# An S5 layer on one Trainium2 core: T products moved between the state inputs, a scan of every fourth step with expansion, and E fetched earlier

## The chip, the cores and the metric

The kernel runs on one core of a Trainium2 chip. The metric is the time of the program on the device in microseconds (us). TensorE (PE) multiplies matrices, VectorE (DVE) and ScalarE (ACT) work element by element on 128 partitions, GpSimd (POOL) does a few side jobs, SyncE (SP) issues nearly all DMA transfers, one after the other in program order. Every engine has its own in-order stream, and semaphores join the streams.

## The reference, cut to what matters

The reference is a network of two blocks over 512 tokens of width 1024. The first block (sparse and dilated attention, cross attention, MLP) and the odd layer of the second are not touched by the change. The part in question is the S5 layer of the even mixer, a linear recurrence in both directions over 256 context and 512 latent steps, for 48 groups of 16 channels and 64 complex states:

```python
def s5_direction(u, lam_re, lam_im, log_step, b_re, b_im, c_re, c_im):
    ...
    lam_bar = jnp.exp(lam * step)
    bu = lax.complex(jnp.einsum('btgh,gph->btgp', u, b_bar.real),
                     jnp.einsum('btgh,gph->btgp', u, b_bar.imag))
    a = jnp.broadcast_to(lam_bar, bu.shape)
    _, s = lax.associative_scan(_linear_recurrence, (a, bu), axis=1)
    return (jnp.einsum('btgp,ghp->btgh', s.real, c_re.astype(f32))
            - jnp.einsum('btgp,ghp->btgh', s.imag, c_im.astype(f32)))
```

Then `even_branch_out` applies gelu and a gated product to the sum of both directions, an FFT mix to the other 256 channels (`ub`), multiplies by `silu(z)` and projects with `even_w_out`.

## The kernel before, in words

The kernel works on chunks of 8 steps, so the recurrence has 96 chunk steps (32 of context, 64 of latents) in each direction. `even` (the S5 layer) runs in this order around the change:

- `U` holds the inputs, three tiles of 16 groups each (a third). They come from transposes of `UC` (L837).
- State inputs ("win products"): 24 pairs of groups `gp`, 16 products each (L1207), of `U` and a weight tile `win` of 512 KB that serves two pairs and is fetched by SP just ahead in the loop (L1201). All results go to banks named `sc`. They are copied into the states `St` by ScalarE (L1213) or, for every odd pair of the first 16, by VectorE (L1211).
- `tree` builds the states of the first 32 chunk steps in five levels of VectorE operations (L1192 to L1195), for 16 pairs at once and then for 8.
- `scan` takes the other 64 chunk steps one by one, 8 VectorE operations of 128x48 each (L1229 to L1235). It is issued at a low priority (`behind(3000)`), so the scheduler, which sets each engine's order when the program is built, lets the weight splits `wlo` (L138) of the products that follow go between its steps.
- Meanwhile TensorE does the product for `ub` (columns 768 to 1024 of `even_w_in`), the four 256-column pieces of the `z` product and the FFT products (`k_dft`).
- `T`: three tiles of 1 MB, the in-chunk response. Each is fetched by 8 DMAs of 16 partitions, in runs of 128 float32 (512 B); they are issued behind the `z` product (L1261). The T products (L1317, 32 matrix instructions in the trace per third) come after the first half of an `even_w_out` product and are copied to `YC` by ScalarE (L1318).
- `E`: six tiles of 1 MB in long runs, fetched inside the loop of the E products (L1333). The E products (L1341) multiply the finished states by `E` and add to `YC` on VectorE (L1346).

The tiles `U`, `UC`, `T`, `E` and `sz` share one pool of nine buffers (`b8`); `win`, `tree`, `YC` and others share a pool of small tiles (`t4`). A load waits until the buffer it reuses has had its last reader, and, since SP's loads report on eight semaphore lanes in turn, until the load that used its lane last has landed. Every weight tile of a product is fetched as `raw` (L131), split into `whi` by ScalarE (L137) and `wlo` by VectorE (L138). A side generator in `self.sides` is advanced by `self.step()`, which `gemm_ch` calls once per weight tile.

Of the kernel before, what the change touches and what calls it, by code (L numbers as in the profile page):

```python
# [83 lines left out]
class Net:  # L84
# [817 lines left out]
    def s5_tables(self):  # L902
# [89 lines left out]
        for j in range(4):  # L992
# [170 lines left out]
    def even(self, hT, U, vpool):  # L1163
# [12 lines left out]

        def tree(g0, gn):

            mt = [self.t4k("tree"), self.t4k("tree")]
            for lev in range(5):  # L1180
                h = 1 << lev
                n = 16 // h
                for d in range(2):
                    m1, m2 = mt[d][:, :4 * n * gn].rearrange("p (k m r g) -> k p m r g", k=2, m=n, r=2)
                    to = lambda t: t.to_broadcast([128, n, 2, gn])
                    if lev:
                        P3 = self.s5P[:, lev - 1, :, d * 24 + g0:d * 24 + g0 + gn]
                        a, b = to(P3[:, None, 0:1]), to(P3[:, None, 1:3])
                    else:
                        a, b = [to(t[:, None, d, :, g0:g0 + gn]) for t in (self.s5A, self.s5B)]  # L1190
                    dst = steps(d, 2 * h - 1, 2 * h, n, g0, gn, False)
                    V.tensor_mul(m1, a, steps(d, h - 1, 2 * h, n, g0, gn, False))  # L1192
                    V.tensor_mul(m2, b, steps(d, h - 1, 2 * h, n, g0, gn, True))
                    V.tensor_add(m1, m1, dst)
                    V.tensor_add(dst, m1, m2)  # L1195

        for gp in range(24):
            o, l = divmod(gp, 8)
            if gp % 2 == 0:
                win = self.t4k("win").rearrange("p (j d r n) -> p j d r n", j=2, d=2, r=2)  # L1200
                nc.sync.dma_start(win, self.WinD[:, gp:gp + 2])  # L1201
            p = self.bank("sc", 2)[:, :384].rearrange("p (r n) -> p r n", r=4)
            for d in range(2):
                for r in range(2):
                    for g in range(2):
                        u = 64 * (g ^ gp % 2)
                        nc.tensor.matmul(p[u:u + 64, 2 * d + r], win[:, gp % 2, d, r, 64 * g:64 * g + 64],  # L1207
                                         U[o][:, 8 * g + l, 32 * d:32 * d + 96], start=True, stop=True)
            dst = St[:, :, :, :, gp].rearrange("p s d r -> p (d r) s")
            if gp % 2 and gp < 16:  # L1210
                V.tensor_copy(dst, p)  # L1211
            else:
                nc.scalar.activation(dst, p, AF.Copy)  # L1213
        tree(0, 16)
        tree(16, 8)

# [8 lines left out]
        mt = self.const.tile([128, 192], F32, name="scan").rearrange("p (d m r g) -> d m p r g", d=2, m=2, r=2)  # L1225
        with self.behind(3000):
            for j in range(32, 96):
                for d in range(2):
                    V.tensor_mul(mt[d][0], self.s5A[:, d], at(d, j - 1))  # L1229
                for d in range(2):  # L1230
                    V.tensor_mul(mt[d][1], self.s5B[:, d], at(d, j - 1, swap=True))
# [22 lines left out]
        self.gemm_ch(hT, W, zc[3:] + zc[:3], e_z)  # L1254
        Ts = []
        for o in range(3):
            T = self.b8("T", (128, 16, 128))
            for k in range(8):
                src = bass.AP(tensor=self.WD.tensor, offset=self.WD.offset + o * 16 * 3840 + (7 - k) * 16,
                              ap=[[240, 16], [3840, 16], [1, 128]])  # L1260
                nc.sync.dma_start(T[k * 16:(k + 1) * 16], src)  # L1261
            Ts.append(T)
        yf = [self.t4.tile([128, 2, 512], F32R, tag="t4", name=self.nm("yf")) for _ in range(2)]
# [44 lines left out]

        YCs = []
        for o, T in enumerate(Ts):  # L1310
            YCs.append(self.t4k("YC").rearrange("p (k l h) -> p k l h", k=8, h=16))
            for l0 in (0, 4):
                p = self.bank("sc", 2).rearrange("p (l n) -> p l n", l=4)
                for l in range(4):
                    for g in range(2):
                        k = 8 * g + l0 + l
                        nc.tensor.matmul(p[64 * g:64 * g + 64, l], U[o][:, k, 32:96], T[:, k], start=True, stop=True)  # L1317
                nc.scalar.activation(YCs[o][:, :, l0:l0 + 4].rearrange("p k l h -> p l k h"),  # L1318
                                     p.rearrange("p l (k h) -> p l k h", h=16), AF.Copy)

        gate = self.row(self.adaD[0, 2 * D:3 * D], self.t4k("gate"))

        self.gemm_tok([(yf[0][:, m], yf[1][:, m]) for m in range(2)], A["even_w_out_2"][0][768:], cols(0, D, 512), self.gated(gate))


        ga = []
        for o in range(3):
            YC = YCs[o]
            for l0 in (0, 4):

                ps = [b[:, :256].rearrange("p (l n) -> p l n", l=2) for b in (self.bank("sc", 2), self.mm())]
                E = self.b8("E", (128, 4, 2, 2, 128))
                nc.sync.dma_start(E, self.ED[:, o * 8 + l0:o * 8 + l0 + 4])  # L1333
                for j0 in (0, 2):
# [183 lines left out]
```

## Time and profile before

| | us |
|---|---|
| median of 3 runs | 1365.66 (1363.42 to 1372.89) |
| the profiled execution | 1365.85 |
| its span from first to last instruction | 1364.1 |
| PE busy, share | 1299.4, 95% |
| DVE busy, share | 987.8, 72% |
| ACT busy, share | 557.0, 41% |
| TensorE clock granted, mean over the span | 0.989 of full |

All times below are microseconds from the start of the span of the profiled execution. In a timeline row the two first numbers are start and length, "xN" says how many instructions are drawn together, and the bracket gives the idle time before the row and what ended it. In a row by windows each engine has its busy time and its instructions; then come the granted clock, the mean busy share of the 16 DMA engines (packets that overlap on an engine can take it above 1) and the rate.

### The profile page before, as it was taken

The page shows a single profiled execution, that of the slowest core. Times are in us where ns is not written, and L with a number is a line of the kernel's source. Part 1 is how long each engine was busy: PE and PEld are TensorE (multiplying, and loading weights), DVE is VectorE, ACT ScalarE, POOL GpSimd, SP SyncE. Part 2 cuts the span into 40 slices and gives each one's busy share as a digit, 9 for nine tenths or more (in the row PEclk, how much of TensorE's full clock was granted, in tenths as well). Part 3 has the DMA queues.
Part 4 walks back from the last instruction along what each step waited for, and adds up shares of the span by engine and source line. Part 5 has one row for each costly group of instructions (what it writes and reads, how often), then busy time and mean ns, then how long its engine had stood idle before and what let it go on. Part 6 is the DMA issues. An engine that isn't in the chain of part 4 may idle for free.

```text
span 1364.1 us, 21183 instructions
## 1 busy us (share of the span) xinstructions
PE 1299.4 (95%) x8106; PEld 1079.8 (79%) x8106; DVE 987.8 (72%) x2284; ACT 557.0 (41%) x992; POOL 71.6 (5%) x135
## 2 busy tenths in 40 slices
PE   5999999999999999999999999979999789999997
PEld 5999577578888888787887887879888678787886
DVE  6998897868966454897999955692499966623545
ACT  5533643554526243433433434552433254333222
POOL 2000000021000010000000001010000000200000
PEclk9999998999999999999999999989999899999999
DMA  6422001055752236534677764551316925321321
GB/s 211 124 63 93 32 1 62 31 183 164 271 203 94 93 74 175 186 108 157 200 210 208 225 197 139 186 152 50 110 54 80 292 94 162 105 93 62 125 92 62
DMA packets 151877, 178.07 MB, mean 131 GB/s; under 512 B 27124, under 2 KB 118490, under 8 KB 151008
## 3 DMA queue, kind: packets, MB, share of 16 engines
q1 hardware_dynamic: 148560, 168.17, 40.3%
q0 software_dynamic: 3216, 8.56, 2.0%
q8 instruction: 64, 1.05, 0.3%
q14 instruction: 37, 0.30, 0.1%
HBM read 161.24 MB, written 15.45 MB: 130 GB/s over the span
## 4 chain that ended last, share of the span: by engine, by line
PE 58%; DVE 9%; ACT 3%; issue 2%; DMA 2%; POOL 1%; SPq 0%; DVEq 0%; POOLq 0%; ACTq 0%
PE mm L175 17%; PE mm L177 16%; PE mm L176 16%; DVE wlo L138 2%; PE pv L682 1%; PE sc L1082 1%; DMA ctx<-ctx_dram 1%; DVE h L317 1%; PE sc L1207 1%; PE tr L299 1%; ACT h L277 1%; PE tr L1064 1%; ACT whi L137 1%; DMA T<-WD 1%; DVE h L319 1%
## 5 line engine op out<-in xcount | busy, mean ns | idle before, releaser
L138 DVE TENSOR_TENSOR wlo<-raw,whi 128x1024 fp32r<-128x1024 f32 (+2 forms) x197 | 230.1, 1185 | 118.4 <-ACT whi L137 118.2
L137 ACT ACTIVATE whi<-raw 128x1024 fp32r<-128x1024 f32 (+2 forms) x197 | 198.5, 1027 | 285.2 <-PE mm L176 114.3
L175 PE MATMUL mm<-hmh,whi 128*128 128x512 f32 (+1 forms) x288 | 106.4, 370 | 0.0
L176 PE MATMUL mm<-hml,whi 128*128 128x512 f32 (+1 forms) x288 | 105.4, 366 | 0.0
L177 PE MATMUL mm<-hmh,wlo 128*128 128x512 f32 (+1 forms) x288 | 105.3, 366 | 0.0
L175 PE MATMUL mm<-whi,ah 128*128 128x512 f32 x256 | 101.3, 398 | 2.3 <-DVE x L618 2.3
L177 PE MATMUL mm<-whi,al 128*128 128x512 f32 x256 | 99.5, 391 | 0.2
L176 PE MATMUL mm<-wlo,ah 128*128 128x512 f32 x256 | 99.4, 390 | 0.0
L175 PE MATMUL mm<-whi,hTh 128*128 128x256 f32 (+1 forms) x304 | 88.3, 290 | 3.5 <-ACT whi L137 2.9
L176 PE MATMUL mm<-wlo,hTh 128*128 128x256 f32 (+1 forms) x304 | 86.8, 286 | 0.0
L177 PE MATMUL mm<-whi,hTl 128*128 128x256 f32 (+1 forms) x304 | 86.6, 285 | 0.0
L618 DVE TENSOR_TENSOR x<-mm,x 128x512 f32<-128x512 f32 x87 | 58.8, 688 | 29.8 <-PE mm L177 29.3
L779 DVE SCALAR_TENSOR_TENSOR adas<-adaw,cond,adas 128x1024 f32<-128x1024 f32 x56 | 70.7, 1280 | 10.4 <-DMA adaw<-ada_w_dram 10.3
L175 PE MATMUL mm<-h2h,whi 128*128 128x512 f32 x160 | 62.8, 392 | 0.0
L176 PE MATMUL mm<-h2l,whi 128*128 128x512 f32 x160 | 62.3, 389 | 0.0
L177 PE MATMUL mm<-h2h,wlo 128*128 128x512 f32 x160 | 62.3, 389 | 0.0
L175 PEld LDWEIGHTS mm<-whi,hTh 128*128 128x128 f32 x304 | 58.6, 193 | 4.6 <-ACT whi L137 3.3
L175 PEld LDWEIGHTS mm<-hmh,whi 128*128 128x128 f32 x288 | 54.3, 189 | 9.6 <-issue 1.0
L175 PEld LDWEIGHTS mm<-whi,ah 128*128 128x128 f32 x256 | 48.0, 188 | 17.3 <-DVE x L618 4.7
L177 PEld LDWEIGHTS mm<-hmh,wlo 128*128 128x128 f32 x288 | 54.3, 189 | 8.9
L176 PEld LDWEIGHTS mm<-hml,whi 128*128 128x128 f32 x288 | 54.4, 189 | 8.4
L176 PEld LDWEIGHTS mm<-wlo,hTh 128*128 128x128 f32 x304 | 58.4, 192 | 1.6 <-issue 1.5
(515 smaller groups left out, 3302.1 us busy)
## 6 DMA issues: line engine op xcount, KB each, us to landing
adaw<-ada_w_dram SPq DMA_DIRECT2D x48, 512.0 KB
raw<-w_up_dram SPq DMA_DIRECT2D x16, 1024.0 KB
raw<-w_down_dram SPq DMA_DIRECT2D x16, 1024.0 KB
raw<-odd_w_in_dram SPq DMA_DIRECT2D x12, 1024.0 KB
raw<-w_in_dram SPq DMA_DIRECT2D x11, 1024.0 KB
raw<-w_kv_cross_dram SPq DMA_DIRECT2D x8, 1024.0 KB
raw<-even_w_in_dram SPq DMA_DIRECT2D x8, 1024.0 KB
WinD<-wst SPq DMA_DIRECT2D x24, 256.0 KB
```

The costliest lines, as they stand in the source:

```text
L137: nc.scalar.activation(hi[:, k], raw[:, k], AF.Copy)
L138: nc.vector.tensor_sub(lo[:, k], raw[:, k], hi[:, k].bitcast(F32))
L175: nc.tensor.matmul(out, lh, rh, start=(first and i == 0), stop=False)
L176: nc.tensor.matmul(out, lh, rl, start=False, stop=False)
L177: nc.tensor.matmul(out, ll, rh, start=False, stop=(final and i == n - 1))
L277: nc.scalar.activation(junk, x, AF.Square, scale=1.0 / math.sqrt(n), accum_out=ss)
L299: nc.tensor.transpose(p[:, k], h[:, (k0 + k) * 128:(k0 + k + 1) * 128], self.ident)
L317: nc.vector.scalar_tensor_tensor(h, x, r, g, op0=OP.mult, op1=OP.mult)
L319: nc.vector.tensor_add(h, h, shift)
L618: self.nc.vector.tensor_add(self.x[i][:, c:c + n], p, self.x[i][:, c:c + n])
L682: nc.tensor.matmul(o[0][:, 2 * (h % 2) + k], self.vc[:, j, c:c + 128], pt[:, j * 128:(j + 1) * 128], start=(j == 0), stop=(j == 1))
L779: nc.vector.scalar_tensor_tensor(acc[v], w, cond[:, v, k:k + 1], acc[v], op0=OP.mult, op1=OP.add)
```

## The change

The loop over the 24 pairs now holds more. All results are copied by ScalarE. Every odd pair uses a bank of the `mm` kind. After each 4 pairs `join(0, ...)` adds to every second step its left neighbour times the transition (8 operations of 128x384), after each 8 pairs `join(1, ...)` does the same for every fourth step with sums of two; 72 operations in all. After each 8 pairs the T products of that third follow at once. T tiles 0 and 1 are issued ahead of the loop, T tile 2 behind pair 13, the first three E tiles behind the loop, the other three behind the `z` product. The scan covers only every fourth step (23 steps of 8 operations with the same 128x48 shape, the transition taken to its fourth power) and runs as a side generator in pieces; then an expansion in three pieces fills the steps between (24 operations of 128x256 and 24 of 128x512). One `self.step()` is added to the FFT loop, and what is left of the generator is drained ahead of the E products. The powers of the transition are kept for two levels instead of four, in another pool; the `t4` pool has 13 buffers instead of 12; a scratch area for software DMAs is set to 8192.

```diff
-        self.t4 = P("t4", 12)
+        self.t4 = P("t4", 13)
...
-        self.s5P = self.t4k("s5P")[:, :576].rearrange("p (j r n) -> p j r n", j=4, r=3)
+        self.s5P = self.const.tile([128, 288], F32, name="s5P").rearrange("p (j r n) -> p j r n", j=2, r=3)
...
-        def tree(g0, gn):
-            mt = [self.t4k("tree"), self.t4k("tree")]
-            for lev in range(5):
...
+        def join(lev, j0, n, g0, gn):
+            h = 1 << lev
+            for d in range(2):
+                m1, m2 = jt[d][:, :4 * n * gn].rearrange("p (k m r g) -> k p m r g", k=2, m=n, r=2)
...
+                dst = steps(d, j0, 2 * h, n, g0, gn, False)
+                V.tensor_mul(m1, a, steps(d, j0 - h, 2 * h, n, g0, gn, False))
+                V.tensor_mul(m2, b, steps(d, j0 - h, 2 * h, n, g0, gn, True))
+                V.tensor_add(m1, m1, dst)
+                V.tensor_add(dst, m1, m2)
+        def t_load(o):
+            T = self.b8("T", (128, 16, 128))
+            for k in range(8):
...
+                nc.sync.dma_start(T[k * 16:(k + 1) * 16], src)
+        def e_load(n):
+            E = self.b8("E", (128, 4, 2, 2, 128))
+            nc.sync.dma_start(E, self.ED[:, 4 * n:4 * n + 4])
+        Ts = [t_load(o) for o in range(2)]
         for gp in range(24):
...
-            p = self.bank("sc", 2)[:, :384].rearrange("p (r n) -> p r n", r=4)
+            p = (self.mm() if gp % 2 else self.bank("sc", 2))[:, :384].rearrange("p (r n) -> p r n", r=4)
...
-            if gp % 2 and gp < 16:
-                V.tensor_copy(dst, p)
-            else:
-                nc.scalar.activation(dst, p, AF.Copy)
-        tree(0, 16)
-        tree(16, 8)
+            nc.scalar.activation(dst, p, AF.Copy)
+            if gp % 4 == 3:
+                join(0, 1, 48, gp - 3, 4)
+            if l == 7:
+                join(1, 3, 24, gp - 7, 8)
+                T = Ts[o]
...
+                            nc.tensor.matmul(p[64 * g:64 * g + 64, l], U[o][:, k, 32:96], T[:, k], start=True, stop=True)
...
+            if gp == 13:
+                Ts.append(t_load(2))
+        Es = [e_load(n) for n in range(3)]
...
-        with self.behind(3000):
-            for j in range(32, 96):
...
+        def scan():
+            for j in range(7, 96, 4):
...
+                if j % 32 == 7:
+                    yield
+            yield
+            for g0 in (0, 8, 16):
+                join(1, 33, 16, g0, 8)
+                join(0, 32, 32, g0, 8)
+                yield
+        self.sides.append(scan())
...
         self.gemm_ch(hT, W, zc[3:] + zc[:3], e_z)
-        Ts = []
-        for o in range(3):
-            T = self.b8("T", (128, 16, 128))
...
+        Es += [e_load(n) for n in range(3, 6)]
...
             wh, wl = self.wload(A["k_dft"], 4, (a, b))
+            self.step()
...
-        YCs = []
-        for o, T in enumerate(Ts):
...
+        for _ in self.sides.pop():
+            pass
...
-    nc = bacc.Bacc("TRN2", target_bir_lowering=False, num_devices=1)
+    nc = bacc.Bacc("TRN2", target_bir_lowering=False, num_devices=1, dynamic_dma_scratch_size=8192)
```

The first place is SP's order of loads. Before, from the last `win` tiles of the loop (`win_9563` and `win_9585` serve pairs 20 to 23) to the first E tile:

```order
L1201 DMA win_9563<-WinD 128x1024
L1201 DMA win_9585<-WinD 128x1024
L131 DMA raw_10452<-even_w_in_dram 128x8x256
L131 DMA raw_10512<-even_w_in_dram 128x8x256
L131 DMA raw_10615<-k_dft_dram 128x4x258
L131 DMA raw_10652<-k_dft_dram 128x4x256
L131 DMA raw_10780<-even_w_out_dram 128x2x512
L1261 DMA T_10572<-WD 16x16x128 x8
L1261 DMA T_10581<-WD 16x16x128 x8
L1261 DMA T_10590<-WD 16x16x128 x8
L131 DMA raw_10826<-even_w_out_dram 128x2x512
L1333 DMA E_10874<-ED 128x2048
```

Now, from the second `win` tile (pairs 2 and 3) on; `win_9405` serves pairs 4 and 5, `win_9569` pairs 14 and 15, `win_9628` pairs 16 and 17:

```order
L1215 DMA win_9375<-WinD 128x1024
...
L1201 DMA T_9335<-WD 16x16x128 x8
L1201 DMA T_9344<-WD 16x16x128 x8
L1215 DMA win_9405<-WinD 128x1024
L1215 DMA win_9427<-WinD 128x1024
L131 DMA raw_10152<-even_w_in_dram 128x8x256
...
L1215 DMA win_9538<-WinD 128x1024
L1201 DMA T_9560<-WD 16x16x128 x8
L1215 DMA win_9569<-WinD 128x1024
L1206 DMA E_9761<-ED 128x2048
L1215 DMA win_9628<-WinD 128x1024
```

Two T tiles now stand between the `win` tiles of pair 3 and pair 4, one between those of pair 13 and pair 14, and an E tile between those of pair 15 and pair 16. The second T tile (`T_9344`) waits for the last transpose of the third `U` tile (`tr_9318` below), because it takes the buffer of the `UC` tile that this transpose reads; the third (`T_9560`) waits for the T products of the first third (`mm_9476` below), whose T tile it replaces.

The second place is TensorE's order. Before, the T products stood behind the first half of `even_w_out` (its last product is the first row):

```order
L177 MATMUL mm_10806<-whi_10781,yf_10600 128x512
L1317 MATMUL sc_10716<-T_10572,U_8664 64x128 x8
L1317 MATMUL sc_10726<-T_10572,U_8664 64x128 x8
L1317 MATMUL sc_10737<-T_10581,U_8665 64x128 x8
L1317 MATMUL sc_10747<-T_10581,U_8665 64x128 x8
L1317 MATMUL sc_10758<-T_10590,U_8666 64x128 x8
L1317 MATMUL sc_10768<-T_10590,U_8666 64x128 x8
L1341 MATMUL sc_10872<-E_10874,St 64x128 x16
```

Now, from pair 1 to pair 8 (L1221 are the state inputs, L1238 the T products):

```order
L1221 MATMUL mm_9365<-U_8654,win_9353 64x96 x2
L837 MATMUL tr_9308<-ident,UC_9199 128x64 x8
L837 MATMUL tr_9318<-ident,UC_9199 128x64 x8
L1221 MATMUL mm_9365<-U_8654,win_9353 64x96 x6
L1221 MATMUL sc_9377<-U_8654,win_9375 64x96 x8
L1221 MATMUL mm_9387<-U_8654,win_9375 64x96 x8
L1221 MATMUL sc_9407<-U_8654,win_9405 64x96 x8
...
L1221 MATMUL mm_9439<-U_8654,win_9427 64x96 x8
L1238 MATMUL mm_9466<-T_9335,U_8654 64x128 x8
L1238 MATMUL mm_9476<-T_9335,U_8654 64x128 x8
L1221 MATMUL sc_9488<-U_8655,win_9486 64x96 x8
```

The T products of a third now follow its eight pairs, and the transposes that free the second T tile's buffer stand inside pair 1, where they stood before too.

## Rows read from the trace of the kernel before

**Rows 1.** By windows, from the last state inputs to the first E products.

```profile
core 0: us, PE busy (x) PEld busy (x) DVE busy (x) ACT busy (x) POOL busy (x), PEclk, DMA share, GB/s
984.00:1080.00 96.00, 85.55 (x605) 73.22 (x603) 95.19 (x612) 35.04 (x58) 3.60 (x7) 0.96 0.57 107
```

**Rows 2.** Waits of PE, 960 to 1104: us in total, times, longest.

```profile
PE sc L1317 <- DMA raw<-even_w_out_dram: 4.3, 1, 4.3
PE sc L1341 <- DVE St L1235: 2.0, 1, 2.0
PE sc L1341 <- issue: 1.0, 1, 1.0
PE mm L175 <- DVE gt L1133: 0.7, 1, 0.7
```

**Rows 3.** Timeline of PE: state inputs, behind z, T products, last E product.

```profile
967.45 1.05 PE L1207 MATMUL sc<-U,win 128*64 128x96 f32 x20
968.44 1.22 PE L837 MATMUL tr<-ident,UC 64*128 64x64 f32 x16
980.67 10.01 PE L1207 MATMUL sc<-U,win 128*64 128x96 f32 x176 [0.15 <-DVE St L1211]
...
1045.18 1.05 PE L1275 MATMUL tr<-fw 128*128 128x128 f32 x8
...
1065.55 3.76 PE L1317 MATMUL sc<-T,U 128*64 128x128 f32 x64
1073.58 3.26 PE L1317 MATMUL sc<-T,U 128*64 128x128 f32 x32 [4.27 <-DMA raw<-even_w_out_dram]
...
1102.41 0.29 PE L1341 MATMUL mm<-E,St 64*64 64x128 f32 x1
```

**Rows 4.** Timeline of SP's queue: the issue of loads.

```profile
927.55 50.77 SPq L1201 DMA_DIRECT2D win<-WinD  x6
...
1042.43 21.73 SPq L1261 DMA_DIRECT2D T<-WD  x24
1064.64 0.39 SPq L131 DMA_DIRECT2D raw<-even_w_out_dram  x1
1065.98 11.20 SPq L1333 DMA_DIRECT2D E<-ED  x6
```

**Rows 5.** By windows (columns as in Rows 1): clock, DMA share, rate.

```profile
960.00:970.00 10.00, 10.00 (x109) 9.66 (x109) 2.37 (x4) 3.20 (x7) 0.00 (x0) 1.00 0.00 0
980.00:982.00 2.00, 1.84 (x42) 1.56 (x38) 1.02 (x2) 0.84 (x1) 0.00 (x0) 1.00 0.96 338
908.00:912.00 4.00, 2.67 (x12) 2.70 (x13) 3.94 (x5) 0.00 (x0) 0.00 (x0) 0.50 0.59 167
1044.00:1062.00 18.00, 14.25 (x85) 12.27 (x85) 17.66 (x115) 7.91 (x19) 0.57 (x1) 0.96 1.27 117
1066.00:1072.00 6.00, 3.31 (x60) 2.98 (x56) 6.00 (x51) 2.39 (x4) 0.00 (x0) 1.00 1.23 130
1072.00:1090.00 18.00, 13.74 (x118) 11.72 (x120) 18.00 (x82) 2.14 (x3) 0.00 (x0) 0.91 1.02 406
```

**Rows 6.** Timeline of DVE: two tree operations; one step of the scan apart.

```profile
984.31 0.69 DVE L1192 TENSOR_TENSOR tree<-s5A,St 128x512 f32<-128x512 f32 x1
984.92 0.68 DVE L1193 TENSOR_TENSOR tree<-s5B,St 128x512 f32<-128x512 f32 x1
...
1069.84 0.33 DVE L1235 TENSOR_TENSOR St<-scan 128x48 f32<-128x48 f32 x2
...
1070.80 0.33 DVE L1235 TENSOR_TENSOR St<-scan 128x48 f32<-128x48 f32 x2
```

**Rows 7.** Groups by line on ACT, 967 to 1104: busy, mean ns | idle before.

```profile
L1213 ACT ACTIVATE St<-sc 128x384 f32<-128x384 f32 x16 | 13.7, 856 | 7.8 <-PE sc L1207 7.3
```

**Rows 8.** Timeline of PE: two waits ahead of the stretch.

```profile
852.96 0.30 PE L299 MATMUL tr<-ident,h 128*128 128x128 f32 x1 [1.47 <-DVE h L319]
...
909.33 0.55 PE L175 MATMUL mm<-whi,cxh 128*128 128x256 f32 x1 [6.46 <-DVE UC L813]
```

More of the change, by code (lines that the diff above doesn't have):

```diff
@@ L987, in s5_tables @@
         V.tensor_copy(self.s5B[:, :, 1], l8[:, 1])
-        self.s5P = self.t4k("s5P")[:, :576].rearrange("p (j r n) -> p j r n", j=4, r=3)
+        self.s5P = self.const.tile([128, 288], F32, name="s5P").rearrange("p (j r n) -> p j r n", j=2, r=3)
         re, im = sw[:, 0], sw[:, 1]
         x = t[:, :48]
-        for j in range(4):
+        for j in range(2):
             a, b, c = (self.s5P[:, j, k] for k in range(3))
@@ L1175, in steps @@
             return bass.AP(tensor=fl.tensor, offset=fl.offset + a + (24 if swap else 0), ap=ap)
-        def tree(g0, gn):
-            mt = [self.t4k("tree"), self.t4k("tree")]
-            for lev in range(5):
[L1181 to L1188, printed above, removed]
-                    else:
[L1190 to L1195, printed above, removed]
+        jt = [self.t4k("join") for _ in range(2)]
@@ new lines, in join @@
+        def join(lev, j0, n, g0, gn):
+            h = 1 << lev
+            for d in range(2):
+                m1, m2 = jt[d][:, :4 * n * gn].rearrange("p (k m r g) -> k p m r g", k=2, m=n, r=2)
+                to = lambda t: t.to_broadcast([128, n, 2, gn])
+                if lev:
+                    P3 = self.s5P[:, lev - 1, :, d * 24 + g0:d * 24 + g0 + gn]
+                    a, b = to(P3[:, None, 0:1]), to(P3[:, None, 1:3])
+                else:
+                    a, b = [to(t[:, None, d, :, g0:g0 + gn]) for t in (self.s5A, self.s5B)]
+                dst = steps(d, j0, 2 * h, n, g0, gn, False)
[3 more added lines that the diff above has]
+                V.tensor_add(dst, m1, m2)
@@ new lines, in t_load @@
+        def t_load(o):
+            T = self.b8("T", (128, 16, 128))
+            for k in range(8):
+                src = bass.AP(tensor=self.WD.tensor, offset=self.WD.offset + o * 16 * 3840 + (7 - k) * 16,
+                              ap=[[240, 16], [3840, 16], [1, 128]])
+                nc.sync.dma_start(T[k * 16:(k + 1) * 16], src)
+            return T
+        def e_load(n):
+            E = self.b8("E", (128, 4, 2, 2, 128))
+            nc.sync.dma_start(E, self.ED[:, 4 * n:4 * n + 4])
+            return E
@@ L1197, in even @@
+        Ts = [t_load(o) for o in range(2)]
+        YCs = []
         for gp in range(24):
@@ L1209, in even @@
             dst = St[:, :, :, :, gp].rearrange("p s d r -> p (d r) s")
-            if gp % 2 and gp < 16:
-                V.tensor_copy(dst, p)
-            else:
-                nc.scalar.activation(dst, p, AF.Copy)
-        tree(0, 16)
-        tree(16, 8)
+            nc.scalar.activation(dst, p, AF.Copy)
[4 more added lines that the diff above has]
+                T = Ts[o]
+                YCs.append(self.t4k("YC").rearrange("p (k l h) -> p k l h", k=8, h=16))
+                for l0 in (0, 4):
+                    p = self.mm().rearrange("p (l n) -> p l n", l=4)
+                    for l in range(4):
+                        for g in range(2):
+                            k = 8 * g + l0 + l
+                            nc.tensor.matmul(p[64 * g:64 * g + 64, l], U[o][:, k, 32:96], T[:, k], start=True, stop=True)
+                    nc.scalar.activation(YCs[o][:, :, l0:l0 + 4].rearrange("p k l h -> p l k h"),
+                                         p.rearrange("p l (k h) -> p l k h", h=16), AF.Copy)
+            if gp == 13:
+                Ts.append(t_load(2))
+        Es = [e_load(n) for n in range(3)]
         def at(d, j, swap=False):
@@ L1225, in even @@
         mt = self.const.tile([128, 192], F32, name="scan").rearrange("p (d m r g) -> d m p r g", d=2, m=2, r=2)
-        with self.behind(3000):
-            for j in range(32, 96):
+        A4 = [self.s5P[:, 1, :, d * 24:d * 24 + 24] for d in range(2)]
+        def scan():
+            for j in range(7, 96, 4):
                 for d in range(2):
-                    V.tensor_mul(mt[d][0], self.s5A[:, d], at(d, j - 1))
+                    V.tensor_mul(mt[d][0], A4[d][:, 0:1].to_broadcast([128, 2, 24]), at(d, j - 4))
                 for d in range(2):
-                    V.tensor_mul(mt[d][1], self.s5B[:, d], at(d, j - 1, swap=True))
+                    V.tensor_mul(mt[d][1], A4[d][:, 1:3], at(d, j - 4, swap=True))
                 for d in range(2):
@@ L1306, in even @@
             self.split(*self.nat(t, yf[0][:, m], yf[1][:, m]))
-        YCs = []
-        for o, T in enumerate(Ts):
[L1311 to L1319, printed above, removed]
         gate = self.row(self.adaD[0, 2 * D:3 * D], self.t4k("gate"))
         self.gemm_tok([(yf[0][:, m], yf[1][:, m]) for m in range(2)], A["even_w_out_2"][0][768:], cols(0, D, 512), self.gated(gate))
+        for _ in self.sides.pop():
+            pass
         ga = []
```

8 lines of the change are left out of this document (1 added, 7 removed).

## The prediction, made blind

> **What bounds the kernel now.** The page comes first: TensorE is the busiest engine by far over the span (table above). So a change pays only where TensorE waits, and costs wherever it makes TensorE wait. The windows of the layer in question show why the average misleads: from 984 to 1080 VectorE is busy for 95.2 of 96 us, TensorE for 85.6 [rows 1]. Then the waits of TensorE in that layer: 4.3 us ahead of the last T products, put down to a weight load, 2.0 us ahead of the first E product for the last scan step, 1.0 and 0.7 us behind it [rows 2]. The timeline gives the places: state inputs from 967.45 to 990.7 without a DMA wait, T products at 1065.55 and 1073.58, the last E product ending at 1102.7 [rows 3]. I count the result as the shift of that end; what follows it is the same work. All durations come from one profiled execution of 1365.85 us (span 1364.1), 0.2 us from the median 1365.66.
>
> **What the change takes away.** Between 1065.55 and the second `even_w_out` half stand T products of 3.76 + 3.26 us and waits of 4.27, 2.0 and 0.7 [rows 2, 3]: 14.0 us. The E tiles, issued from 1065.98 on [rows 4], are there earlier, so the 1.0 us wait goes too; later E tiles can bring another 0 to 2, and I take 1: 16 us. From the end of the state inputs (980.67 + 10.01 = 990.7) to the last E product (1102.7) [rows 3] are 112 us; 96 are left (95 to 97).
>
> **What it adds on TensorE.** The T products now stand among the state inputs. The 64 at full clock took 3.76 us [rows 3], so 96 take 5.6. Without any new wait the phase would end at 990.7 + 5.6 = 996.3 and the E products at 1092.3, 10.4 us earlier.
>
> **What it adds on VectorE.** An operation of 128x512 takes 0.61 us of its queue (984.31 to 984.92), a scan step of eight 128x48 operations 0.96 (1069.84 to 1070.80), so 0.12 each [rows 6]. Between these, 128x384 is 0.475 and 128x256 0.34. Joins: 72 x 0.475 = 34 us. Scan: 23 x 0.96 = 22. Expansion: 24 x 0.34 + 24 x 0.61 = 23. Sum 79. Before: eight copies, the tree (984.3 to 1003.1) and 64 x 0.96 = 61 of scan, about 87. VectorE saves 8 us and can begin at about 972 instead of 984, since joins start behind four pairs. The states are then ready about when the FFT products end, not behind them: the 2.0 us wait has its cover. The copies all go to ScalarE at 0.86 us [rows 7], less than the 0.91 us of a pair (176 instructions, 11 pairs, in 10.0 us [rows 3]): nothing, as long as no weight split of ScalarE's falls between two; if one does, a pair is late by about 1 us, within the range.
>
> **What it adds on SP's queue.** This decides. `win` loads were issued long ahead (six by 978.3 [rows 4]), and TensorE never waited for one. Now two T tiles stand ahead of the one for pair 4. How long is a T tile of 1 MB? While T tiles fill the queue the 16 DMA engines show a share of 1.23 to 1.27, that is full, at 117 and 130 GB/s, while the E tiles run at 406 with a share of 1.02, and `win` reached 338 [rows 5]. So 8.1 to 9.0 us per T tile, 2.6 per E tile, 1.6 per `win` of 512 KB. And later loads stand behind: the 512 KB issued at 1064.64 [rows 4] released TensorE only at 1073.58 [rows 3], when T had drained.
>
> *First stop.* T tile 0 takes the buffer of an earlier `UC` tile and runs through the quiet stretch ahead (share 0.00 from 960 to 970 [rows 5]). T tile 1 reuses a `UC` tile whose last transpose ends at 968.44 + 1.22 = 969.7 [rows 3]. Its issue takes 8 x 0.45, data flow about 1.5 us after the first issue (issues from 1042.43, a full queue from 1044 [rows 4, 5]): 971.2 to 979.3 or 980.2. `win` of pair 4 lands at 981 to 982. TensorE has done pairs 0 to 3 and the transposes at 967.45 + 4 x 0.91 + 1.2 = 972.3. It stands 8.5 to 9.5 us.
>
> *Second stop.* T tile 2 waits for the T products of the first third: 981.5 + 4 x 0.91 + 1.9 = 987, up to 989 at a low clock. On the ring stand one `win`, a 1 MB weight tile and three `win` (3.1 MB at 338 to 406 GB/s: until 989 to 991), then T tile 2 until 997 to 1000, then `win` of pair 14 at 999 to 1001.6. TensorE comes there at 992.5 to 994.5. It stands 5.5 to 8 us. The `win` of pair 16 lies behind an E tile: 2.6 + 1.6 us later, while TensorE has 1.8 + 1.9 us of work: 0.5 us.
>
> The three stops, 9 + 6.8 + 0.5 = 16.3 us at the middle (14.5 to 18), put the end of the phase at 1012.6 and that of the E products at 1108.6 instead of 1102.7. VectorE loses nothing by it. The last pair ends 1.9 us of T products ahead of 1012.6, and its copy (0.86) and 16 joins (7.6) end at 1019.2; nine scan steps (8.6) and a weight split of 2048 columns (4 x 0.61 = 2.4) end at 1030. That split, for the second piece of `z`, stands behind those nine steps in VectorE's order. The product for `ub` and the four pieces of `z` have as many columns each and fill 990.7 to 1045.2 [rows 3], 10.9 us each: TensorE needs the split at 1012.6 + 21.8 = 1034.4.
>
> **Elsewhere.** The second context tile no longer waits for a buffer that the first holds, so the 1.47 us wait at 852.96 [rows 8] may go: 0 to 1.5, taken as 1. Smaller powers, another pool, the scratch size: no instruction on this path, nothing.
>
> **The sum.** -10.4 + 16.3 - 1 = +4.9: 1365.85 + 4.9 = 1371, and 1367 to 1374 with the bounds above (stops 14.5 to 18, rest 95 to 97, context 0 to 1.5).
>
> **The rivals.**
>
> *No stop, or half.* If T tiles move faster than the rows say, or the `win` packets overtake them, up to 15 us of the stops go: 1365.85 - 10.4 - 1 = 1354, with other waits among the E products gone 1351. For it: before, T shared the queue with other loads in part of its time. Against it: even with little else the rate was 117 to 130 GB/s. [...]
>
> *VectorE becomes the bound.* The first joins read and write in runs of four numbers; the tree had 8 and 16, which no row here tells for four. If such an operation took twice as long (0.95), the 64 of them that follow pair 7 (first third done at 986) would end at 1047 instead of 1019, the split for the second `z` piece at 1058, and TensorE, needing it at 1034, would stand some 20 us at most, since later splits keep the same distance: 1391, slower. It decides from about 0.59 us per operation on (986 + 64 x 0.59 = 1024, and 11 us to the split). Against it: the tree's two widths differ as their element counts do. [...]
>
> [...]
>
> **Chances.** Both stops (1363 to 1376) 0.54; one or both halved (1357 to 1363) 0.13; none (1349 to 1356) 0.17, half of it under 1352; stops with clock (1376 to 1384) 0.10, half of it above 1379.3; VectorE 0.06. The range 1354 to 1380 leaves out about 0.2. Faster or slower by 1% (13.7 us, what a measurement of this kernel can tell): faster 0.09, slower 0.11, same 0.80.
>
> **What would show it.** In the trace after: the state inputs stretched from 23 us to 40 or more, with TensorE waiting on the DMA of `win` ahead of pairs 4 and 14; `win` landing right behind T; a DMA share above 1 at some 120 GB/s near 971 to 980; no T products behind `even_w_out`; the E products without the 4.3 and 2.0 us waits; VectorE's joins near 0.475 us. I am wrong if `win` lands within 2 us of its need (then 1354), or if a weight split on VectorE is waited for in the `z` product.

## The result: 0.9% slower, and the profile after

| | before | changed |
|---|---|---|
| median of the runs | 1365.22 us (1363.25 to 1372.89) | 1376.87 us (1374.02 to 1384.69), 7 runs |
| the profiled execution, its span | 1365.85, 1364.1 | 1375.64, 1373.5 |
| TensorE clock granted, mean | 0.989 | 0.982 |

The ratio is 1.009, with a 95% interval of 1.0069 to 1.0112. The forecast was 1371 in a range of 1354 to 1380, "same" within 1%. The time lies in the range, but 0.9 us above the likeliest case (1363 to 1376) and in the band of the rival "stops with clock" (1376 to 1384, chance 0.10). In the profiles the shift is +9.4 us where the sum had +4.9.

The waits of TensorE from 960 to 1104 in the changed kernel (us in total, times, longest) answer to [rows 2]:

```profile
PE sc L1221 <- DMA win<-WinD: 19.8, 3, 10.6
PE mm L176 <- DVE wlo L138: 3.5, 1, 3.5
PE mm L175 <- ACT yf L309: 0.3, 1, 0.3
```

The four old waits are gone. The loads of `win`, which TensorE never waited for, now stop it three times. The timeline of TensorE shows where [rows 3, 8 answer to it]; L1221 are the state inputs, L1238 the T products, L1307 the first work behind `z`, the last row is the first work of the next layer:

```profile
850.50 1.11 PE L299 MATMUL tr<-ident,h 128*128 128x128 f32 x4 [2.28 <-DVE cxl L310]
...
969.92 0.88 PE L1221 MATMUL sc<-U,win 128*64 128x96 f32 x16
...
984.73 1.55 PE L1221 MATMUL sc<-U,win 128*64 128x96 f32 x16 [10.64 <-DMA win<-WinD]
...
989.88 2.09 PE L1238 MATMUL mm<-T,U 128*64 128x128 f32 x32
991.78 0.84 PE L1221 MATMUL sc<-U,win 128*64 128x96 f32 x16
992.44 0.84 PE L1221 MATMUL mm<-U,win 128*64 128x96 f32 x16
...
995.26 0.88 PE L1221 MATMUL sc<-U,win 128*64 128x96 f32 x16 [0.65 <-DMA win<-WinD]
...
1005.31 1.55 PE L1221 MATMUL sc<-U,win 128*64 128x96 f32 x16 [8.51 <-DMA win<-WinD]
...
1073.30 1.05 PE L1307 MATMUL tr<-fw 128*128 128x128 f32 x8
...
1080.83 0.38 PE L176 MATMUL mm<-wlo,ub 128*128 128x256 f32 x1 [3.48 <-DVE wlo L138]
...
1171.95 1.06 PE L299 MATMUL tr<-ident,h 128*128 128x128 f32 x8 [0.71 <-DVE h L319]
```

The stops stand ahead of pairs 4, 12 and 14 (a row of 16 instructions is a pair; pair 8 starts at 991.78). The queue of SP says why [rows 4]: two `win` tiles are out by 903, the next two leave behind both T tiles, the one for pair 12 is the last of the three behind a weight tile, and the one for pair 14 leaves behind the third T tile.

```profile
900.06 2.61 SPq L1215 DMA_DIRECT2D win<-WinD  x2
...
959.40 16.50 SPq L1201 DMA_DIRECT2D T<-WD  x16
975.94 0.96 SPq L1215 DMA_DIRECT2D win<-WinD  x2
977.75 0.38 SPq L131 DMA_DIRECT2D raw<-even_w_in_dram  x1
978.95 4.28 SPq L1215 DMA_DIRECT2D win<-WinD  x3
992.00 4.92 SPq L1201 DMA_DIRECT2D T<-WD  x8
996.97 0.45 SPq L1215 DMA_DIRECT2D win<-WinD  x1
```

By windows (columns as in [rows 1], the clock third from the end): T goes at 118 GB/s with a full share, in the first stop the clock falls to 0.50, and ahead of the layer it is 0.57 behind the new wait on `cxl`.

```profile
850.00:854.00 4.00, 3.50 (x13) 3.08 (x14) 2.62 (x4) 1.20 (x2) 0.00 (x0) 0.57 0.58 186
964.00:966.00 2.00, 2.00 (x19) 2.00 (x19) 0.43 (x1) 0.38 (x1) 0.00 (x0) 1.00 1.26 118
980.00:982.00 2.00, 0.00 (x0) 0.00 (x0) 0.00 (x0) 0.00 (x0) 0.00 (x0) 0.50 1.32 125
984.00:1080.00 96.00, 83.46 (x737) 75.28 (x737) 82.42 (x305) 38.06 (x57) 3.04 (x6) 0.91 0.53 164
```

Against [rows 1] VectorE is busy for 82 of the 96 us instead of 95, TensorE for 83 instead of 86: the work taken off VectorE became idle time. By stretches of TensorE's timeline:

| stretch | before | changed | difference | predicted |
|---|---|---|---|---|
| start to state inputs | 967.45 | 969.92 | +2.5 | -1 |
| state inputs to the end of `z` | 77.7 | 103.4 | +25.7 | +21.9 |
| end of `z` to the next layer's first transposes | 117.4 | 98.7 | -18.7 | -16 |
| sum | | | +9.4 | +4.9 |

The next layer's transposes start at 1162.56 in the kernel before; the sum is also the difference of the two spans. The last E product ends at 1117.35 instead of 1102.70.

### The profile page after: what moved, and what is told of

Read it like the earlier page. It is cut to its first block, busy times and chain, and to the rows that moved or that the text cites. A ratio compares the mean times of both kernels' runs of the same rounds, so it can differ in the third digit from the quotient of the medians.

```text
span 1373.5 us, 20841 instructions
## 1 busy us (share of the span) xinstructions
PE 1298.5 (95%) x8106; PEld 1082.3 (79%) x8106; DVE 979.5 (71%) x1978; ACT 561.5 (41%) x1000; POOL 71.9 (5%) x135
## 4 chain that ended last, share of the span: by engine, by line
PE 67%; DVE 19%; DMA 4%; ACT 4%; issue 3%; POOL 1%; SPq 1%; DVEq 0%; POOLq 0%; ACTq 0%
PE mm L175 17%; PE mm L177 17%; PE mm L176 17%; DVE wlo L138 3%; PE pv L601 2%; PE tr L586 2%; DVE m L539 1%; DMA win<-WinD 1%; PE sc L577 1%; PE sc L573 1%; DVE acc L540 1%; DMA raw<-w_in_dram 1%; PE pv L682 1%; ACT whi L137 1%; DMA ctx<-ctx_dram 1%
```

## The experiments

Ratios are against the kernel before, measured beside each run. Several edits keep TensorE's order of work; where not, it is said.

**The states alone.** T and E stay where they were; joins, scan of every fourth step and expansion are those of the change.

```diff
-        Ts = [t_load(o) for o in range(2)]
...
-                T = Ts[o]
...
         self.gemm_ch(hT, W, zc[3:] + zc[:3], e_z)
+        Ts = [t_load(o) for o in range(3)]
```

> The changed kernel with T and E loads and the T products put back to where the kernel before has them (T loads behind the z product, T products ahead of the gate, E loads inside the E loop); joins, scan of every fourth step and expansion stay. Theory 'queue' (T and E tiles ahead of the win loads make the three stops): no DMA wait in the state inputs, which take 23 to 24 us again. But the stops had also given VectorE 19 us of rest, and the split of the second FFT weight stands behind the expansions, so TensorE waits there 8 to 14 us instead of 3.5; the 4.3 us wait ahead of the last T products and the 2.0 us one ahead of E shrink. 1371 us (1367 to 1374). Rival 'states' (the new VectorE and ScalarE work itself stretches the state inputs): the state inputs stay near 48 us and the time at 1377. Rival 'states are a gain by themselves': 1363 to 1366.

1386.75 us, ratio 1.0141 (1.0118 to 1.0164): a miss of 16 us, and slower than the whole change. TensorE's waits and SP's queue in it:

```profile
PE sc L1335 <- DMA raw<-even_w_out_dram: 7.9, 1, 7.9
PE sc L1219 <- DMA win<-WinD: 7.7, 1, 7.7
PE mm L177 <- DVE wlo L138: 5.8, 1, 5.8
PE tr L1372 <- ACT ga L1373: 3.5, 1, 3.5
```

```profile
901.15 2.61 SPq L1213 DMA_DIRECT2D win<-WinD  x2
910.62 66.53 SPq L131 DMA_DIRECT2D raw<-even_w_in_dram  x3
977.21 13.37 SPq L1213 DMA_DIRECT2D win<-WinD  x10
```

With no T tile in front, `win` of pair 4 still comes 7.7 us late. The third of the three weight loads waits until about 977 for VectorE to have read the buffer that it takes, and ten `win` tiles stand behind it. The waits of SP's queue name it (the longest of the three is the one that counts):

```profile
SPq L131 <- DVE wlo L138: 72.0, 3, 56.6
```

So the first stop has two causes: what is in front (T, or a load that waits for a buffer), and that only two `win` tiles are out before it. Moving T and E, the other half of the change, wins back 10 us by medians and 7 by the ratios.

**T's bytes.** First two of the three tiles are not fetched (zeros in their place), then all three are fetched in 8 KB runs (other data), then in 128 partitions. The order of ScalarE's instructions is that of the change in all three, and VectorE's too, but for a few operations that swap places in the first.

```diff
+            if o:
+                nc.gpsimd.memset(T, 0.0)
-            for k in range(8):
+            for k in range(0 if o else 8):
```

> The changed kernel with the loads of T tiles 1 and 2 left out (GpSimd fills them with zeros, so two thirds of the in-chunk response are missing from the output). 'Queue': the 10.6 and 8.5 us stops go, the state inputs with the T products take about 29 to 33 us instead of 48; VectorE is then late and the wait for the split of the second FFT weight grows from 3.5 to about 12. 1363 us (1359 to 1367). Blind prediction's no-stop case, in which VectorE costs nothing: 1357 with the 2.5 us that came ahead of the layer. Rival 'states': 1372 or more.

1356.74 us, ratio 0.9932 (0.991 to 0.9954). Two stops of 3.2 and 1.6 us remain, and the wait on the second `k_dft` split is 4.6 instead of 3.5. Expected were 1363 by the queue and 1357 without a stop. The time is the second's, though stops are left; the wait of about 12 us for VectorE, on which the 1363 rested, did not come.

```diff
-                src = bass.AP(tensor=self.WD.tensor, ..., ap=[[240, 16], [3840, 16], [1, 128]])
+                src = bass.AP(tensor=self.WD.tensor, ..., ap=[[1024, 16], [1, 2048]])
```

> The changed kernel with the same 24 T loads of 128 KB at the same places, but each partition's 8 KB read as one run instead of 16 runs of 512 B (the T data are then others, so the output is not the reference's). 'Queue, by run length': a T tile takes about 2.6 us instead of 8 to 9, the first stop about 5 us, the second about 3, the DMA share falls to about 1 at 400 GB/s; the wait for the second FFT weight grows by some us: 1367 us (1363 to 1370). Rival 'by number of DMAs' or by the issue of 24 loads: the stops stay within 1 us of 10.6 and 8.5, 1377.

1372.85 us, ratio 1.0043 (1.0027 to 1.006); three stops, 14.9 us. Runs of 8 KB instead of 512 B take 5 of 19.8 us, no more: the time lies between the theory's 1367 and the rival's 1377, and neither holds.

```diff
+                        nc.gpsimd.dma_start(self.TD[k * 16:(k + 1) * 16, o * 16:(o + 1) * 16], src)
...
-                nc.sync.dma_start(T[k * 16:(k + 1) * 16], src)
+                nc.sync.dma_start(T[:, g:g + 2], self.TD[:, o * 16 + g:o * 16 + g + 2])
```

> The changed kernel, with the order of every engine unchanged; only the shape of T's loads differs: the three tiles are laid out once, in the MLP stage, in a table TD in DRAM (24 copies from DRAM to DRAM, issued by GpSimd), and each is then fetched by 8 DMAs of 128 partitions in runs of 1 KB, where it was 8 DMAs of 16 partitions. Long runs alone (8 KB, still 16 partitions) had left T at 127 to 152 GB/s. Theory 'width': a DMA that writes 16 partitions is slow whatever its runs, so a T tile now goes like E, 2.6 us. Then the win of pair 4, issued at about 976, lands at 979 instead of 984.7, and the first stop is 4 us; T tile 2 costs 1.6 us ahead of pair 14; 14 us of the 19.8 us of stops go, 2 us of half clock with them, and the later wait for the second k_dft split grows by 1: 1360 us (1357 to 1363). Rival 'source': T stays slow because of what else is on the queue or because of the number of DMAs: the stops stay, 1373 to 1376.

1372.05 us, ratio 1.0022 (1.0005 to 1.004), 12 us above the theory and 1 us under the rival's range, whose reason (T stays slow) is out. Half of the theory's premise was right: T goes faster, though not at E's rate. Windows of the first T tile (columns as before), first in 8 KB runs of 16 partitions, then in this kernel, then in `both_12` below, where a tile is one DMA:

```profile
964.00:966.00 2.00, 2.00 (x19) 2.00 (x19) 0.24 (x1) 0.38 (x1) 0.00 (x0) 1.00 1.03 127
```

```profile
964.00:966.00 2.00, 2.00 (x19) 2.00 (x18) 0.43 (x1) 0.38 (x1) 0.00 (x0) 1.00 0.84 259
```

```profile
964.00:966.00 2.00, 2.00 (x19) 2.00 (x18) 0.42 (x1) 0.21 (x1) 0.00 (x0) 1.00 0.98 414
```

118 (512 B runs), 127, 259 and 414 GB/s: 128 partitions in runs of 1 KB were twice as fast as 16 in runs of 8 KB. From 259 to 414 the author's estimate of the limit is SP's issue of eight DMAs (a median of 0.45 us each in the changed kernel, so 3.6 us for 1 MB), with the share at 0.84 where the rate is 259; but the runs grow from 1 to 8 KB as well, and the two were not told apart. The stops are still 6.9 and 5.1 us:

```profile
984.43 1.55 PE L1224 MATMUL sc<-U,win 128*64 128x96 f32 x16 [6.92 <-DMA win<-WinD]
1001.00 1.55 PE L1224 MATMUL sc<-U,win 128*64 128x96 f32 x16 [5.12 <-DMA win<-WinD]
```

`win` left SP at 979.26 in it and released TensorE 5.2 us later. T tile 1 cannot start before the last transposes, and `win` stands behind its eight issues and its data.

**`win` ahead of T.**

```diff
+        wins = [w_load(gp) for gp in range(0, 8, 2)]
         Ts = [t_load(o) for o in range(2)]
...
-                nc.sync.dma_start(win, self.WinD[:, gp:gp + 2])
+                win = wins.pop(0)
+                if gp + 8 < 24:
+                    wins.append(w_load(gp + 8))
```

> The changed kernel with four win tiles issued ahead of the T tiles, and each later one four steps earlier, T's loads as they were: SP issues six win tiles, then T tiles 0 and 1, five win tiles, T tile 2, the last win tile. Theory 'queue': pairs 0 to 11 no longer stand behind T; only pairs 22 and 23 can, by 3 us at most. The phase of state inputs and T products ends near 1001 instead of 1018, the half clock goes, the k_dft wait grows by 1: 1358 us (1355 to 1361). Rival 'VectorE floor': joins 34, scan 22, expansion 23 and the splits and sums between, 12 us, are 91 us that begin at 974.5 at the earliest and so end at 1066 at best (1083 in the changed kernel): of the 19.8 us no more than 10 come back, 1366, with a wait on a VectorE split in the z product.

1361.61 us, ratio 0.9956 (0.9939 to 0.9973): 15 us under the change, with T as narrow as before; 10.7 us of stops are left, 7.4 of them ahead of the last tile, the only one that still stands behind T tile 2:

```profile
984.87 11.52 SPq L1201 DMA_DIRECT2D T<-WD  x8
997.30 0.34 SPq L1211 DMA_DIRECT2D win<-WinD  x1
```

The price of that row was set at 3 us; the other 3 us of stops, ahead of tiles that leave right behind T tile 1, were not foreseen. No split is waited for in `z`, and the `k_dft` wait is down to 0.3 us: the rival's 1366 falls.

Next the same with 12 buffers of `t4` in place of 13:

```diff
-        self.t4 = P("t4", 13)
+        self.t4 = P("t4", 12)
```

> As win_ahead, with 12 buffers in the t4 pool as before the change instead of 13; the order of TensorE ahead of this layer is then that of the kernel before, but for the transposes of the second context tile, which still come earlier. Theory 'pools, thirteenth buffer': the shift of 2.5 to 4 us ahead of the layer goes, 3 us below win_ahead: 1355. Rival 'pools, the place of s5P': the shift comes from the context tile that no longer waits for its buffer, and it stays: equal to win_ahead within 1 us.

1359.1 us, ratio 0.9944 (0.9923 to 0.9965). The interval overlaps that of `win_ahead`, so the difference alone settles nothing; the wait on `cxl` is 2.28 us in both, which speaks for the rival.

**Both.** T from `TD` in one DMA per tile, and five `win` tiles ahead (still 12 buffers).

```diff
+            nc.sync.dma_start(T, self.TD[:, o * 16:o * 16 + 16])
-        wins = [w_load(gp) for gp in range(0, 8, 2)]
+        wins = [w_load(gp) for gp in range(0, 10, 2)]
```

> Five win tiles ahead of T, T tiles fetched from TD in one DMA of 128 partitions each, 12 buffers in t4. Theory 'queue': no stop at all, the phase ends at 998 to 1000: 1352 us (1350 to 1355). Rival 'VectorE floor': TensorE then waits for VectorE's splits by what the queue gave back, no better than win_ahead_12.

1357.68 us, ratio 0.9924 (0.9896 to 0.9953). TensorE does not wait for `win` at all. The theory's 1352 is missed all the same, and the rival's "no better than `win_ahead_12`" holds within the intervals. TensorE waits elsewhere, on ScalarE's copy of the `ub` product, which waits for VectorE:

```profile
1013.74 0.79 PE L175 MATMUL mm<-hlh,whi 128*128 128x512 f32 x1 [6.58 <-ACT ubf L1297]
```

```profile
1013.30 0.38 ACT L1297 ACTIVATE ubf<-mm 128x256 f32<-128x256 f32 x1 [4.10 <-DVE ub L310]
```

So the stops are made of both: narrow T with `win` behind it gives 19.8 us, wide T (eight DMAs) 12.0, narrow T with four `win` tiles ahead 10.7, T in one DMA with five ahead 0. And VectorE is next: its joins run without a gap until about 1012 in `both_12`.

**The floor under it.** Three kernels on top of `both_12`. First one tile for all pieces of `ubf`, which takes no further buffers:

```diff
+        ubf = self.t4k("ubf")
-            t = self.t4k("ubf")[:, :n]
+            t = ubf[:, i * n:i * n + n]
```

> both_12 with one tile for the four ubf pieces, each piece in its own quarter, so that ScalarE's copies of the ub product no longer wait for VectorE to have read the piece before; in both_12 TensorE stood 6.6 us at 1013.7 on that copy, because VectorE was at the joins until 1011.5. Theory 'VectorE floor': TensorE then runs into VectorE at the next place: the split for the second z piece stands behind 9 scan steps and ended at 1024.3 in both_12, TensorE wants it at 995.4 + 21.8 = 1017.2 and stands 7 us: 1357.5 us, equal to both_12 within 1. Rival 'one buffer': the wait goes and nothing takes its place: 1351.

1353.55 us, ratio 0.9926 (0.9897 to 0.9955; the profiled run 1352.09), between the two. TensorE waits at the place that was named, for 4.2 us where 7 were forecast:

```profile
1019.75 0.66 PE L177 MATMUL mm<-hlh,wlo 128*128 128x512 f32 x1 [4.21 <-DVE wlo L138]
```

Next, beside that, the scan as late as its consumers let it be:

```diff
-        self.sides.append(scan())
+        with self.behind(3000):
+            for _ in scan():
+                pass
```

> ub_free with scan and expansion issued at the low priority that the scan had before the change, so that the splits of the z pieces go ahead of them on VectorE: the split for the second z piece follows the joins and ends near 1014.5. Theory 'VectorE floor': the joins begin at 976 at the earliest, and joins 34, sums of ub 1.4, splits 7, scan 22, expansion 23 and k_dft splits 3.7 follow one another until 1067; TensorE comes to the second k_dft split at 1057 and stands up to 5 us there or ahead of the E products: 1354 us (1352 to 1356). Rival 'order alone': with the splits early nothing is late, 1350 to 1351.

1358.33 us, ratio 0.9945 (0.9926 to 0.9965), not faster. The wait moved from the `z` split to the second `k_dft` split, at the same price:

```profile
1063.66 0.58 PE L176 MATMUL mm<-wlo,ub 128*128 128x256 f32 x1 [4.35 <-DVE wlo L138]
```

That is what a bound by VectorE's total looks like: from the first join (982.73) to 1069.6 VectorE has no gap, and in `ub_free` none from 974.67 to 1065.6. The medians differ by 4.8 us with overlapping intervals, the two profiled executions (1352.09 and 1363.46) by 11.4. Of these, 8.0 us stand ahead of the layer: the same product starts at 841.19 and at 849.18, and the clock of the second was 0.50 for 13.7 us from 147.3 on, in work that no edit touches. From there to the next layer's transposes the late scan costs 3.4 us in these profiles (307.8 and 311.2; `both_12` takes 310.4).

Last, the subtractions of the splits in `z` on GpSimd:

```diff
+        self.lo = nc.gpsimd
         self.gemm_ch(hT, W, zc[3:] + zc[:3], e_z)
+        self.lo = V
```

> ub_free with the low parts of the four z weight tiles (eight subtractions of 128x1024, 2.35 us for two on VectorE) computed by GpSimd, which is idle there; VectorE is left with joins, sums of ub, scan, expansion and the k_dft splits. Theory 'VectorE floor': the wait of 4.2 us ahead of the second z piece, which stood behind joins and nine scan steps on VectorE, goes, VectorE ends 7 us earlier, and no wait takes its place: 1349 us (1348 to 1351). Rival 'GpSimd late': no row shows GpSimd at an operation of this size (a memset of 128x1024 took 0.95 us); if one takes over 5.4 us, half of a z piece's 10.9 us, TensorE waits for GpSimd at each piece: 1357 or more, and if the two engines hinder each other VectorE's joins and scan steps come out longer than 0.47 and 0.96 us.

1368.8 us, ratio 1.0007 (0.9991 to 1.0024): the rival, in its second form. GpSimd takes 2.4 us per operation (4.76 us for the two of the second row below; 7.02 for the two of the first), early enough, but single operations of VectorE come out longer meanwhile. GpSimd, then VectorE, in the same 20 us:

```profile
1010.27 7.02 POOL L139 TENSOR_TENSOR wlo<-raw,whi 128x1024 fp32r<-128x1024 f32 x2 [31.25 <-ACT whi L138]
...
1022.70 4.76 POOL L139 TENSOR_TENSOR wlo<-raw,whi 128x1024 fp32r<-128x1024 f32 x2
```

```profile
1012.29 2.75 DVE L1200 TENSOR_TENSOR St<-join 128x384 f32<-128x384 f32 x1
1014.96 2.40 DVE L1271 TENSOR_TENSOR scan<-s5P,St 128x48 f32<-128x48 f32 x1
...
1022.04 5.50 DVE L1275 TENSOR_TENSOR St<-scan 128x48 f32<-128x48 f32 x2
```

A join takes 2.75 us instead of 0.55, one scan operation 2.40 and two 5.50, where two took 0.33. TensorE then waits 8.6 and 6.5 us for the `k_dft` splits.

**The shift ahead of the layer.** The kernel before with the pools of the change, then with `s5P` alone moved (12 buffers); both have the change's smaller scratch for DMAs:

```diff
-        self.t4 = P("t4", 12)
+        self.t4 = P("t4", 13)
...
-        self.s5P = self.t4k("s5P")[:, :576].rearrange(...)
+        self.s5P = self.const.tile([128, 576], F32, name="s5P").rearrange(...)
```

> The kernel before with the three changes of memory alone: the powers in the pool of constants, 13 small buffers instead of 12, the scratch size 8192. Theory 'pools' (they reorder work ahead of the layer): about 2.5 us slower, 1367.7, with the wait of TensorE at 850 on the context's transposes and the clock near 0.57 behind it. Otherwise 1365, and the 2.5 us come from the layer's own code as the scheduler sees it.

1371.0 us, ratio 1.0034 (1.0018 to 1.0049): slower, as the theory says, by 4.2 us instead of 2.5 (the interval reaches from 2.5 to 6.7). The wait is there (2.24 us at 851.18), and the clock is 0.58 and 0.57 from 852 to 856.

> The kernel before the change with one edit, s5P in the const pool instead of a t4 buffer (and the scratch size of the change, without which it does not fit). TensorE's order differs from the kernel before in one place, the transposes of the second context tile, which come earlier by 18 groups. Theory 'place of s5P': this is the shift ahead of the layer: TensorE waits 2.3 us on cxl, the clock halves behind it, and the kernel is 2.5 to 4 us slower than before: ratio 1.002 to 1.003. Rival 'thirteenth buffer': the shift came with the t4 pool of 13, and this kernel equals the one before: ratio 0.999 to 1.001.

1370.06 us, ratio 1.0022 (1.001 to 1.0035), with the wait that the changed kernel has at 850.50:

```profile
854.32 0.66 PE L299 MATMUL tr<-ident,h 128*128 128x128 f32 x4 [2.24 <-DVE cxl L310]
```

The forecast half clock behind the wait is not there: the clock is 1.00 from 854 to 860. The freed `t4` buffer lets the second context tile be normed earlier, and the scheduler puts its transposes 18 groups earlier into TensorE's stream. Their operand `h` is ready there; what is not free are the two banks `tr` that they write to, until VectorE has read the first tile's transposes out of them (`cxl`). The rows of VectorE in the changed kernel, where TensorE stands until 850.50:

```profile
844.84 1.22 DVE L319 TENSOR_TENSOR h<-h,shift 128x1024 f32<-128x1024 f32 x1
...
849.44 1.95 DVE L310 TENSOR_TENSOR cxl<-tr,cxh 128x512 fp32r<-128x512 f32 x2
```

From 841 to 909 the profile of `s5p_const` is 1.2 us longer than that of the kernel before, from 841 to the next layer's transposes 2.6 us (`pools_only` 2.4); the medians differ by 3.3. What makes up the rest of the 2.6 us was not placed. Whether the thirteenth buffer adds to it is open (the two intervals overlap), and the smaller scratch was not tried by itself.

**The fastest of these** are `both_12` and `ub_free`: the change with `win` ahead, T in one DMA and 12 buffers, the second with one `ubf` tile as well. By ratios (0.9924, 0.9926) they are not told apart; by medians they are 9.9 and 13.2 us under the runs of the kernel before that were made beside each. The longest wait of TensorE that is left in the layer is for VectorE in both (6.6 us by way of `ubf`, 4.2 us).

## Why the prediction was right, point by point

- **Elsewhere: failed.** "The 1.47 us wait at 852.96 may go" was forecast as -1; it came out as +2.5. The context tile does start earlier, as said, but its transposes then wait 2.28 us for their banks, and the clock is 0.57 for 4 us behind it, which is 1.7 us of work. "Another pool: nothing" was the false step: a freed buffer changes the order that the scheduler sets. Of the 2.5 us, 0.9 stand already ahead of the context tile (one product starts at 842.05 instead of 841.19) and say nothing about it.
- **The stops: right in kind and place, 3.5 us short.** 19.8 us against 16.3. First 10.64 (8.5 to 9.5 said), second 8.51 (5.5 to 8), third 0.65 (0.5), the third ahead of pair 12 and not of pair 16. Of the first stop's 1.6 us, half is that TensorE came 0.7 us sooner (4.2 us after the start of the state inputs, where the working has 4.85), by the shorter pairs of the next point. The price of T held: 118 GB/s against the 117 and 130 of [rows 5]. That T gets its buffer when the last transpose ends held too (the end at 972.13, the first load of T tile 1 at 972.16).
- **The pairs: a term was left out on each side.** A pair takes 0.66 us now (991.78 to 992.44) where it took 0.91 [rows 3]; 24 of them are 6.0 us less. That TensorE has five banks instead of two is the author's guess at the cause; no run tests it by itself. The trace of the kernel before rules out VectorE's copies as the cause: its last eight pairs are copied by ScalarE alone too, and still take 0.93 us each.

```profile
984.21 7.42 ACT L1213 ACTIVATE St<-sc 128x384 f32<-128x384 f32 x8 [0.98 <-PE sc L1207]
```

  The half clock behind the stops took it back: four pairs took 5.15 us (984.73 to 989.88, at a granted clock of 0.50) instead of 2.6, pairs 14 and 15 and the T products behind them 5.7 (1005.31 to 1011.0, at 0.53) instead of 3.2, so 5.0 us. Stops 19.8, T products 5.6, half clock 5.0 and pairs -6.0 make 24.4 of the 25.7 us of that stretch. That is the rival "stops with clock" of the chances, in time and in cause. The rows had shown such a fall, 0.50 behind a wait of 6.46 us [rows 5, 8]; in the changed kernel the clock is 0.50 from 977 to 990 and from 1002 to 1008, in the two long stops and behind them. That the sum came as near as 4.5 us is in part luck: the 6.0 and the 5.0 us, neither of them in it, nearly cancel.
- **What is taken away: right, and more.** -18.7 us against -16. T products of 7.0 and the waits of [rows 2] went. The sum had left out two waits of the kernel before that went too, 2.67 us on `yf` and 3.65 us on `ga` (the rows below). The first stands in the view of [rows 2], between the first two lines shown there; the second is behind its window. Left out too was the clock: it had been 0.50 for 3.4 us each from 1060.4, 1074.1 and 1108.2 on, at the waits on `yf`, the weight load and `ga`, and the changed kernel has one such fall in this stretch (1082.4).

```profile
1059.45 0.50 PE L175 MATMUL mm<-whi,yf 128*128 128x512 f32 x1 [2.67 <-ACT yf L309]
...
1108.08 1.04 PE L1354 MATMUL tr<-ident,YC 128*128 128x128 f32 x4 [3.65 <-ACT ga L1355]
```

- **A new wait, not foreseen at its place.** 3.48 us at 1080.83, where the kernel before had 1.08: the second `k_dft` split stands in VectorE's order among the last expansion operations. "VectorE saves 8 us" held for its work, but it lost 18 us waiting for ScalarE's copies (11.55 and 6.40) while TensorE stood.
- **VectorE's price of a join: right.** The first two operations of the first join, whose runs are of four numbers:

```profile
975.57 0.56 DVE L1191 TENSOR_TENSOR join<-s5A,St 128x384 f32<-128x384 f32 x1 [0.82 <-ACT St L1224]
976.04 0.55 DVE L1192 TENSOR_TENSOR join<-s5B,St 128x384 f32<-128x384 f32 x1
```

0.47 us apart, as worked out from [rows 6], and those with runs of eight are the same (1025.60 to 1026.07). So the rival of 1391 is out. (By its own numbers, 1058 and 1034, that rival had 24 us and not 20, so 1395.)
- **T's rate: the row had it right.** Runs of 8 KB did not help much. Few partitions were slow: 106 to 131 GB/s in 16 partitions with runs of 512 B (the changed kernel from 962 to 968, 974 to 982 and 996 to 1002) and 127 to 152 with 8 KB (`t_long_runs`), against 414 in 128 (`both_12`), each in windows of 2 us. Why 16 partitions were slower than 128 no run shows.

## What to carry to other kernels

Before a load is put ahead of a loop's own loads, look at what it waits for (the loads behind it on the queue waited too: ten `win` tiles in `states_only`, until 977.21) and at how many of the loop's tiles are already out; here `win` issued ahead was worth 15 us by medians with T unchanged. Where loads are late, look at width before run length: here 128 partitions in one DMA gave 3.5 times the rate of 16 in eight (414 against 118 GB/s), and long runs alone 1.1 times (127). Work that is taken off an engine pays only where that engine was waited for (here VectorE was busy for 82 of 96 us instead of 95, and the kernel 0.9% slower), and a freed buffer can move work elsewhere (2.24 us of wait on `cxl` in `s5p_const`), so compare the order of the whole program, not only of the part that was edited.

## What the runs showed of the hardware that was not expected

- A tile of 1 MB, from 964 to 966: 118 GB/s in 8 DMAs of 16 partitions and 512 B runs, 127 in 8 KB runs, 259 in 8 DMAs of 128 partitions and 1 KB runs, 414 in one DMA of 128 partitions and 8 KB runs.
- In `z_pool`, while GpSimd was at operations on two operands of 128x1024, single VectorE operations on two operands came out longer: 2.75 us for 0.55, 2.40 for 0.20, 5.50 for two that took 0.33. GpSimd was busy for 21.2 us with the eight, and VectorE was 14.6 us longer at joins and scan than in `ub_free` (scan operations 41.8 us for 29.8, joins of 128x384 35.6 for 33.0).
- In the profiled executions of `low_scan` and `s5p_const` the granted clock was 0.50 for 13.7 us from 147.3 on; in those of `ub_free` and of the kernel before it was 1.00 there. TensorE had done the same in all four (from 140 to 147 it was busy for 6.7 us). So at 841 `low_scan` is 8.0 us behind `ub_free`, and `s5p_const` 4.7 us behind the kernel before. What brings it on is open. The runs of `ub_free` alone spread from 1352.09 to 1362.19 us, so it may come and go between executions of one kernel; that was not traced.
